# Upsampling by two: three rows moved from the third load to the first

## The chip, the cores and the metric

The kernel runs on one core of a Trainium2 chip. The metric is the device time of one execution in microseconds (us). The core has a VectorE (DVE) and a ScalarE (ACT) that compute here, a SyncE (SP) whose queue issues all transfers, a GpSimd (POOL) that only closes the program, and 16 DMA engines that carry the bytes between HBM (device memory) and the on-chip memory of 128 partitions.

## The reference

The input `x` is float32 of shape (16, 64, 64, 64). Every element is repeated twice along the height and twice along the width, so the output has shape (16, 64, 128, 128):

```python
for i in range(new_h):
    for j in range(new_w):
        result[:, :, i, j] = x[:, :, i // 2, j // 2]
```

Nothing is computed; 16.78 MB are read and 67.11 MB are written.

## The kernel before

Batch, channel and height together are 65,536 rows of 64 elements (256 B). Each of the 128 partitions takes 512 consecutive rows (`R = 512`), so in HBM a partition's input is one run of 128 KiB, and its output, four times as long, another one. One input row becomes two output rows of 128 elements, 1,024 B.

**Memory.** One tile, `mem`, holds everything in a partition: a work area at the front, of `WF` = 79 x 256 elements (room for 79 expanded rows), and behind it the whole input, `xt`, of 512 x 64 elements.

**Loads.** The input comes in three transfers on SP's queue (L195), cut at the rows `[0, HEAD, R // 2 + HEAD, R]`. With `HEAD = 32` they take 32, 256 and 224 rows of each partition: 8,192, 65,536 and 57,344 B a partition. `begin_before_barrier` moves their issue ahead of the program's start barrier.

**Chunks.** The 512 rows are expanded in nine chunks, `rows = [54, 38, 54, 61, 54, 63, 63, 63, 62]`. For each chunk VectorE copies the first `kv` rows (L213) and ScalarE the others (L214), each with a broadcast source that names every element four times; then SP issues one store of the chunk (L215). In the first chunk VectorE takes all rows but one (53 of 54), in the others about five eighths. Even chunks are expanded at the front of `mem`; odd chunks so that they end where their own source begins, over input rows that have been used up.

**What orders the work.** The program's waits are drawn from the overlap of what each step reads and writes in `mem`. The first chunk reads rows 0 to 53, which are in the first and the second load, so it waits for both. The second chunk is written over rows that the first chunk reads, so ScalarE's part of it waits for VectorE's first copy. Each later chunk waits until the store of the chunk two before it has landed, as it is expanded into the same space. The third load is first needed by the sixth chunk. All twelve transfers are on one queue, so on each DMA engine they follow each other in the order of issue: three loads, then nine stores. `close_early` lets the program's closing steps run while the last store is under way; at the very end SP waits for the last store alone.

Of the kernel before, what the change touches and what calls it, by code (L numbers as in the profile page):

```python
# [153 lines left out]
@with_exitstack  # L154
def kernel(
    ctx: ExitStack,
    tc: tile.TileContext,
    x: bass.AP,
    scale_factor: int,
    out: bass.AP,  # L160
):
    nc = tc.nc
    nc.at_finalize(begin_before_barrier)
    nc.at_finalize(close_early)
    P = nc.NUM_PARTITIONS
    s = int(scale_factor)
    B, C, H, W = x.shape
    R = B * C * H // P
    fdt = x.dtype

    xp = x.rearrange("b c h w -> (b c h) w").rearrange("(p r) w -> p r w", p=P)
    op = out.rearrange("b c (h hd) w -> (b c h) (hd w)", hd=s).rearrange(
        "(p r) w -> p r w", p=P
    )

    rows = [54, 38, 54, 61, 54, 63, 63, 63, 62]
    GROW = s * s
    FREE = 79
    WF = FREE * GROW * W
    assert sum(rows) == R
    mem_pool = ctx.enter_context(tc.tile_pool(name="mem", bufs=1))
    mem = mem_pool.tile([P, WF + R * W], fdt, name="mem")
    xt = mem[:, WF:].rearrange("p (r w) -> p r w", r=R)

    HEAD = 32
    cuts = [0, HEAD, R // 2 + HEAD, R]
    for lo, hi in zip(cuts, cuts[1:]):
        nc.sync.dma_start(out=xt[:, lo:hi], in_=xp[:, lo:hi])  # L195

    def expanded(r0, r1):
        return (
            xt[:, r0:r1].unsqueeze(2).unsqueeze(4).to_broadcast([P, r1 - r0, s, W, s])
        )  # L200

    r0 = 0
    before = (0, 0)
    for n, k in enumerate(rows):
        size = k * GROW * W
        at = 0 if n % 2 == 0 else WF + r0 * W - size
        assert at >= before[1] or at + size <= before[0]
        before = (at, at + size)
        u = mem[:, at : at + size].rearrange(
            "p (k a w b) -> p k a w b", k=k, a=s, w=W  # L210
        )
        kv = k - 1 if n == 0 else k * 5 // 8 & ~1
        nc.vector.tensor_copy(out=u[:, :kv], in_=expanded(r0, r0 + kv))  # L213
        nc.scalar.copy(out=u[:, kv:], in_=expanded(r0 + kv, r0 + k))  # L214
        nc.sync.dma_start(out=op[:, r0 : r0 + k, :], in_=u)  # L215
        r0 += k
# [35 lines left out]
```

## Time and profile before

| | |
|---|---|
| median of 3 runs | 197.04 us (196.91 to 197.17) |
| the profiled execution | 196.92 us, of which 195.6 us are the span from first to last instruction |
| VectorE | 9 copies, 52.3 us |
| ScalarE | 9 copies, 40.8 us, and a table load of 1.3 us |
| DMA | 83.89 MB in 1,728 packets, 99.2% of 16 engines' span |
| first load | issued at 0.00 us, landed after 4.7 us |
| second load | landed at 24.01 us |
| first store | issued at 38.48 us, landed at 57.30 us |

Of the 1,728 packets 192 are writes of 4 B to a semaphore, one for each of the 12 transfers on each of the 16 engines; the other 1,536 are one for each partition of each transfer, eight on each engine.

The profile is one execution, taken by the hardware profiler. "L213" is line 213 of the kernel. The page gives busy times of engines and of DMA; a row of digits cuts the span (or the window that was asked for) into 40 slices and gives the busy share of each in tenths, where 9 is 90% or more. The DMA view of a narrow window counts a packet, its bytes and its whole duration at the packet's start, so a share can be over 100%: times the window's length and 16 engines, and divided by the number of packets, it gives the mean duration of one. The chain of waits lists the work that ended last, each piece with its start and its duration in us.

### The profile page before, as it was taken

How to read it: one execution, taken by the hardware profiler on the slowest of the kernel's cores; microseconds unless marked ns; L12 is line 12 of the kernel's file. 1: busy time of each engine (PE TensorE's matmuls, PEld its weight loads, DVE VectorE, ACT ScalarE, POOL GpSimd, SP SyncE). 2: the span in 40 equal slices, each digit the busy share in tenths (PEclk: the TensorE clock that was granted, in tenths of full speed). 3: DMA queues.
4: the chain of work that ended last, by engine and by line, in shares of the span. 5: the costliest groups of instructions: out<-in, count | busy, mean ns of one | idle time of the engine just before them, and what ended most of it. 6: DMA issues, size and time to landing. Idle time of an engine off the chain costs nothing.

```text
span 195.6 us, 102 instructions
## 1 busy us (share of the span) xinstructions
DVE 52.3 (27%) x9; ACT 42.1 (21%) x10; POOL 0.2 (0%) x4
## 2 busy tenths in 40 slices
DVE  0000099940026091053008204500540073000000
ACT  2000000160029700059500004970000073000000
POOL 0000000000000000000000000000000000000000
DMA  9999989889899989999999899999999999999994
GB/s 429 429 429 429 402 375 563 375 362 543 362 436 390 555 362 418 486 409 409 409 420 532 362 531 433 422 422 422 422 422 422 422 422 422 422 435 545 467 428 208
DMA packets 1728, 83.89 MB, mean 429 GB/s; under 512 B 192, under 2 KB 192, under 8 KB 192
## 3 DMA queue, kind: packets, MB, share of 16 engines
q1 hardware_dynamic: 1728, 83.89, 99.2%
HBM read 16.78 MB, written 67.11 MB: 429 GB/s over the span
## 4 chain that ended last, share of the span: by engine, by line
DMA 65%; ACT 11%; DVE 7%; SPq 0%; issue 0%; DVEq 0%; ACTq 0%
DMA out_dram<-mem 53%; DMA mem<-in_x_dram 12%; ACT mem L214 11%; DVE mem L213 7%; SPq L195 0%; DVEq L213 0%; ACTq L214 0%; SPq L215 0%
## 5 line engine op out<-in xcount | busy, mean ns | idle before, releaser
L213 DVE COPY mem<-mem 128x9728 f32<-128x9728 f32 (+3 forms) x9 | 52.3, 5818 | 110.9 <-DMA out_dram<-mem 86.8
L214 ACT COPY mem<-mem 128x6400 f32<-128x6400 f32 (+5 forms) x9 | 40.8, 4530 | 119.4 <-DMA out_dram<-mem 84.2
L214 ACT ACT_TABLE_LOAD x1 | 1.3, 1283 | 1.7 <-PEq L233 1.7
L233 POOL MEMSET const-bfloat16-1.0<- 128x1 bf16 x1 | 0.1, 102 | 0.0
L233 POOL MEMSET const-uint8-127<- 128x1 uint8 x1 | 0.1, 102 | 0.0
L233 POOL MEMSET const-float32-1.0<- 128x1 f32 x1 | 0.1, 99 | 0.0
L233 POOL MEMSET const-float32-0.0<- 128x1 f32 x1 | 0.1, 98 | 0.2 <-issue 0.2
## 6 DMA issues: line engine op xcount, KB each, us to landing
out_dram<-mem SPq DMA_DIRECT2D x3, 8064.0 KB, 32.4
out_dram<-mem SPq DMA_DIRECT2D x3, 6912.0 KB, 22.9
out_dram<-mem SPq DMA_DIRECT2D x1, 7936.0 KB, 32.3
out_dram<-mem SPq DMA_DIRECT2D x1, 7808.0 KB, 29.3
mem<-in_x_dram SPq DMA_DIRECT2D x1, 7168.0 KB, 40.1
out_dram<-mem SPq DMA_DIRECT2D x1, 4864.0 KB, 26.7
mem<-in_x_dram SPq DMA_DIRECT2D x1, 1024.0 KB, 4.7
mem<-in_x_dram SPq DMA_DIRECT2D x1, 23.6
```

What stands on the lines that cost most here:

```text
L213: nc.vector.tensor_copy(out=u[:, :kv], in_=expanded(r0, r0 + kv))
L214: nc.scalar.copy(out=u[:, kv:], in_=expanded(r0 + kv, r0 + k))
L233: nc = _bacc.Bacc("TRN2", target_bir_lowering=False, num_devices=1)
```

## The change

The first load takes 35 rows of each partition instead of 32 (8,960 B instead of 8,192 B), the third 221 instead of 224 (56,576 B instead of 57,344 B). The second keeps its 256 rows but begins and ends three rows later in `x` and in `xt`. Copies, stores, their order and their waits are the same.

```diff
-    HEAD = 32
+    HEAD = 35
     cuts = [0, HEAD, R // 2 + HEAD, R]
     for lo, hi in zip(cuts, cuts[1:]):
         nc.sync.dma_start(out=xt[:, lo:hi], in_=xp[:, lo:hi])
```

## The prediction

> **What bounds the kernel now.** I read the page first, for the load on each resource.
>
> ```profile
> span 195.6 us, 102 instructions
> DVE 52.3 (27%) x9; ACT 42.1 (21%) x10; POOL 0.2 (0%) x4
> DMA  9999989889899989999999899999999999999994
> q1 hardware_dynamic: 1728, 83.89, 99.2%
> HBM read 16.78 MB, written 67.11 MB: 429 GB/s over the span
> ```
>
> The 16 DMA engines are busy for 99.2% of the span, all on one queue; VectorE and ScalarE are idle three quarters of the time. The kernel is bound by bytes through the DMA engines. It moves 83.89 MB before and after the change, so the time can move only if an engine runs dry, if bytes move at another rate, or if the 16 engines share the work less or more evenly. The chain of waits shows where an engine could run dry.
>
> ```profile
> 0.42 23.59 DMA mem<-in_x_dram
> ...
> 24.11 14.30 DVE mem L213
> ...
> 38.48 18.82 DMA out_dram<-mem
> ...
> 57.33 4.89 ACT mem L214
> ...
> 62.24 22.85 DMA out_dram<-mem
> ```
>
> The columns are start and duration. The second load lands at 24.01, VectorE copies 53 rows of the first chunk until 38.41 and the first store is issued at 38.48. The third load has been queued since 0.9 us and fills the DMA engines meanwhile. So the chain through VectorE is not itself the bound: it only has to deliver the first store before the engines finish the third load. How near that is, the DMA view shows in narrow windows. It books each packet at its start. First 39.6 to 41.2 (0.04 us a digit), then 1.0 to 1.5 (0.0125 us a digit), then 2.7 to 3.6.
>
> ```profile
> DMA  0000000000090099999990090900000000000000
> DMA packets 32, 0.88 MB, mean 553 GB/s; under 512 B 16, under 2 KB 16, under 8 KB 16
> ...
> DMA  9990000000900900009000000099909000900090
> q1 hardware_dynamic: 16, 0.13, 126.0%
> ...
> DMA packets 48, 0.39 MB, mean 437 GB/s; under 512 B 0, under 2 KB 0, under 8 KB 0
> q1 hardware_dynamic: 48, 0.39, 103.0%
> ```
>
> In the first window 16 packets are semaphore writes that close the third load, one on each engine, and the other 16 are the first data packets of the first store (16 x 55,296 B = 0.88 MB). The latter start between 40.04 and 40.64: 1.56 us and more after the issue at 38.48. In the second window are the first packets of the very first load, issued at 0.00 on an empty queue: from 1.00 to about 1.48 us after their issue. This is the only place where the trace shows how long an idle engine takes from issue to first packet.
>
> **The change part by part.** *The second load lands later.* Three rows more are 128 x 3 x 256 B = 98.3 KB ahead of it; at 429 GB/s that is 0.23 us. Per engine it is the same: 8 packets grow by 768 B. The landing goes from 24.01 to 24.24, VectorE's copy from 24.11 to 24.34, the first store's issue from 38.48 to 38.71. The 14.30 us of the copy stays (same rows, same shape).
>
> *The third load is shorter by the same 98.3 KB.* It starts 0.23 us later on each engine and ends where it ended: engines come free between 40.04 and 40.64 as before. The sum of load bytes, and the count of packets (three loads of 128), are unchanged: 0.
>
> *The first load's packets grow from 8,192 to 8,960 B.* The steady ones in the third window cost 1.030 x 0.9 us x 16 / 48 = 0.309 us each. The growth is in the 0.23 us already. The first packets cost 1.260 x 0.5 x 16 / 16 = 0.63 us, so 0.32 us of start-up; it falls on the first packet whatever its size, and I take no change for it. Bounds: the packet size would save or cost at most that 0.32 us.
>
> *What of the 0.23 us reaches the end?* The cover is the time between the first store being ready to start and the engines coming free. Ready is not shown by the trace, because the engines were busy. Lower bound of the cover: nothing, if a store's first packet needs the whole 1.56 us. Upper bound: a store might start as soon as SP's issue instruction of 0.35 us is done, which would leave 1.21 us at the earliest engine. The nearest row is the first load's 1.00 to 1.48. If the engine that starts first there is also the one free first here, the cover is 40.04 - 38.48 - 1.00 = 0.56 us; if the slowest one is, it is 40.04 - 38.48 - 1.48 = 0.08 us. Against 0.23 that leaves +0.33 or -0.15 us. Most engines come free later than 40.04, so I take the cover as sufficient: 0 us, and in the worst pairing 0.15 us on an engine that is early anyway.
>
> The Trainium skill ("DMA: Bandwidth & Descriptors", section "Latency and other measured facts") gives about 0.6 us to the first byte for DMAs issued from this queue. By that figure the cover would be 0.96 us, an estimate from the page; no run here shows it for a store, and the loads' 1.00 to 1.48 us is longer.
>
> An engine that does run dry pays more than its gap, if it restarts as it did at the beginning: 0.32 us. With the whole 0.23 us uncovered, that makes 0.55 us on that engine. Whether it shows at the end depends on which engine: the closing semaphore packets of the last store start between 194.77 and 195.21 (eight of 16 before 194.9, two after 195.1), so an early engine has up to 0.44 us to lose.
>
> *What is queued behind the later wait.* On SP, the second store is behind the first; it goes out when ScalarE's 3.61 us copy ends, at 42.1, now 42.3, but its packets are wanted only when the first store's are done, near 56.4: covered by 14 us. ScalarE's copy and VectorE's next one follow the first copy and move by 0.23 us under the same cover. From there every step waits for a store's landing, so it moves with the DMA queue. The least cover I find is that of the third store: issued at 62.24, and wanted when the second is done near 68, as VectorE's next copy, which waits for that landing, starts at 68.89. So 6 us. Sum: 0.00 us on the profiled execution's 196.92 us (span 195.6 and 1.3 around it), which is 0.12 below the median of the runs shown, 197.04. I carry the median over.
>
> **The rivals.**
>
> *Slower: the first store comes too late.* Place: the join of third load and first store, 40.04 to 40.64. It decides from the point where a store needs over 1.33 us (1.56 - 0.23) from issue to first packet. For it: the first load's slowest engine needed 1.48. Against it: every engine has its own time, most come free after 40.2, and the engines that finish last have up to 2.1 us. Price: 0.23 us if all engines wait and restart freely, 0.55 with the start-up of the cold packets: 197.27 to 197.59. Chance 0.17. Of that, 0.10 lies over the 0.39 us that make 0.2%.
>
> *Slower: loads at a worse offset.* The second and third load now begin 8,960 B into each partition's rows, on both sides a multiple of 256 B, no longer of 512 B. Every packet in this trace was a multiple of 512 B at such an offset, so no row prices it. The widest rate difference between packets here is that of 8,192 B in 0.309 us, 26.5 GB/s, against 27.1 for 55,296 B (window 44 to 56: 96 packets with a share of 102.0%, so 1.020 x 12 x 16 / 96 = 2.04 us each): 2.3%. Over the 36.5 us of these two loads that would be 0.84 us; 1% would be 0.37. So 197.4 to 197.88. Against it: the packets stay long and contiguous. Chance 0.16.
> The Trainium skill ("DMA: Bandwidth & Descriptors", section "How a descriptor splits into AXI transactions") says that a transfer is cut into 256-byte pieces, and that only a start off a 256-byte boundary costs extra; all starts and lengths here keep to it, so by that rule this rival's price is nothing. No row of this trace shows it.
>
> *Faster: the engines finish more evenly.* The end is set by the last of 16 engines, at 195.21, while half of them are done before 194.90: 0.31 us to be had if the start-up falls more evenly with longer first packets. The packets that run while the first store is issued cost a little more, too: about 2.14 us each on the mean (window 37.9 to 38.45: 3.883 x 0.55 x 16 / 16) where the ones before took 2.12 (35.8 to 36.4: 3.311 x 0.6 x 16 / 15), together 0.27 us, possibly on few engines; with the last one among them, up to that is saved. Taken together up to 0.58 us, so 196.46; the greater part of it is needed to pass 0.2%. For it: only the spread. Against it: nothing in the change evens anything out. Chance 0.12.
>
> *The change does nothing* is the forecast itself: three rows later and well covered. Chance 0.55.
>
> **How the numbers follow.** The likeliest case is the covered one: 197.04 us, with the runs' own 196.91 to 197.17. About 0.2%, 0.39 us, is what a measurement of this kernel can tell from no change. Faster by more takes most of the faster rival: 0.10. Slower: 0.10 from the late store and 0.14 from the offset, 0.24. Within: 0.55, 0.07 and 0.02 from the two slower rivals and 0.02 from the faster: 0.66. The range takes in the covered case, all of the late store's price and the near halves of the other two: 196.75 to 197.65, which leaves out some 0.15.
>
> **What the profile after would show.** Right: the second load's landing near 24.24, the first store's issue near 38.71, its first packets still from 40.04, each right behind the third load's last one; DMA still at 99%. Late store: a step of more than 0.1 us in the time from which those packets start, and longer first packets. Offset: the third load ends later though the store is in time, at 40.3 or beyond, and its packets take over 2.12 us x 56,576 / 57,344 = 2.09 us. Faster: closing packets nearer together and ending before 194.9. The forecast is wrong if the median leaves 196.75 to 197.65.

## The result and the profile after

The kernel takes 197.54 us after the change (median of 21 runs, 197.38 to 197.92) against 197.16 us before (21 runs beside them, 196.84 to 197.58): a ratio of 1.0019, 95% interval 1.0012 to 1.0026. It is slower by 0.2%, near the bound that the prediction named, and clear of noise. The profiled execution took 197.45 us, with a span of 196.1 us.

The page of the profile after:

```profile
span 196.1 us, 102 instructions
DMA  9999989989899989999999899999999999999994
q1 hardware_dynamic: 1728, 83.89, 99.1%
```

DMA stays the bound, on the same packets and bytes. The chain of waits after (start, duration, what):

```profile
0.42 23.91 DMA mem<-in_x_dram
...
24.43 14.30 DVE mem L213
...
38.80 18.62 DMA out_dram<-mem
...
57.44 4.89 ACT mem L214
...
62.35 22.96 DMA out_dram<-mem
```

The second load lands at 24.33 instead of 24.01 and the first store is issued at 38.80 instead of 38.48: 0.32 us later, where 0.23 was forecast. Then two windows of the DMA view after, each with its count of packets: the join of third load and first store, 39.6 to 41.2 (0.04 us a digit), and the very end, 195.3 to 195.8.

```profile
DMA  0000000000000099990999990090000000000000
DMA packets 32, 0.88 MB, mean 553 GB/s; under 512 B 16, under 2 KB 16, under 8 KB 16
...
DMA packets 2, 0.00 MB, mean 0 GB/s; under 512 B 2, under 2 KB 2, under 8 KB 2
```

The first store's packets still start between 40.1 and 40.7, so the join looks as before. But two of the 16 closing packets now start after 195.3. Before, the last two started between 195.1 and 195.3, the window of these lines:

```profile
DMA  0000000001000000000001000000000000000000
DMA packets 2, 0.00 MB, mean 0 GB/s; under 512 B 2, under 2 KB 2, under 8 KB 2
```

The two late engines of after can be followed in the trace. A packet starts where the one before it on its engine ended, within some 0.01 us, so the records can be strung into 16 chains, one an engine. Before, each engine takes 154.6 us (154.59 to 154.75) from its first store packet to its closing packet, and no engine has a gap at the join. After, 14 engines take 154.6 to 154.7 and close between 194.85 and 195.24. The other two end their third load at 40.30 and 40.47, start their first store packet only at 40.42 and 40.66, and then take 155.1 us: the 0.5 us more are spread over most of their 72 store packets, 7 ns each on the mean. They close at 195.53 and 195.75. Without them the end would be 195.24, as the 195.21 of before. So the difference of these two spans, 0.5 us, lies on two engines: a gap of 0.1 to 0.2 us at the join, and 0.5 us in small pieces over the nine stores. The medians of the two kernels are only 0.38 us apart; the profiled execution of before was one of its quicker ones.

### The profile page after: what moved, and what is told of

It reads as the page before. It is cut to its first block, busy times and chain, and to the rows that moved or that the text cites. A ratio compares the mean times of both kernels' runs of the same rounds, so it can differ in the third digit from the quotient of the medians.

```text
span 196.1 us, 102 instructions
## 1 busy us (share of the span) xinstructions
DVE 52.3 (27%) x9; ACT 42.1 (21%) x10; POOL 0.2 (0%) x4
## 4 chain that ended last, share of the span: by engine, by line
DMA 65%; ACT 11%; DVE 7%; SPq 0%; issue 0%; DVEq 0%; ACTq 0%
DMA out_dram<-mem 53%; DMA mem<-in_x_dram 12%; ACT mem L214 11%; DVE mem L213 7%; SPq L195 0%; DVEq L213 0%; ACTq L214 0%; SPq L215 0%
## 6 DMA issues: line engine op xcount, KB each, us to landing
mem<-in_x_dram SPq DMA_DIRECT2D x1, 7072.0 KB, 40.2
```

## The experiments

The runs were made in four groups, each with its own runs of the kernel before, whose medians were 197.38 to 197.44 us; the row "after" is the result above, beside 197.16 us. So the ratios carry the comparison, not the medians. "Stretch" is by how much the last packet of the third load is longer than the others of its size, mean of 16 engines. "Slow" counts the engines that take over 154.85 us from first store packet to close. Both are from the one profiled execution of each kernel. In e5 and e9 the chains of several engines run so close together that they can be confused, and the count is rough; the sum over all engines is not affected, and there it is 5.2 and 5.0 us over 16 x 154.59, that of ten engines with 0.5 us each.

The expectations call an engine dry that finished its third load before the first store's packet was at hand; such an engine shows a gap. A slow engine need not show one (e9).

| kernel | first store issued, us | stretch, us | slow | median, us | ratio to before (95%) |
|---|---|---|---|---|---|
| 52 rows on VectorE (e11) | 31.57 | 0.91 | 0 | 198.35 | 1.0053 (1.0040 to 1.0067) |
| 49 rows, HEAD 32 (e7) | 37.59 | 0.46 | 0 | 198.00 | 1.0029 (1.0018 to 1.0041) |
| 49 rows, HEAD 35 (e6) | 37.72 | 0.60 | 0 | 197.77 | 1.0019 (1.0010 to 1.0028) |
| HEAD 22 (e13) | 37.80 | 0.45 | 0 | 197.55 | 1.0007 (0.9998 to 1.0016) |
| 51 rows, HEAD 35 (e1) | 38.27 | 0.04 | 0 | 197.30 | 0.9996 (0.9987 to 1.0006) |
| one-row pieces (e8) | 38.31 | 0.18 | 0 | 197.34 | 0.9996 (0.9986 to 1.0005) |
| HEAD 29 (e3) | 38.42 | 0.02 | 0 | 197.16 | 0.9993 (0.9981 to 1.0005) |
| HEAD 30 (e14) | 38.47 | 0.02 | 0 | 197.11 | 0.9988 (0.9979 to 0.9997) |
| before (HEAD 32) | 38.48 | 0.02 | 0 | | 1 |
| larger first load alone (e10) | 38.55 | 0.00 | 0 | 197.39 | 1.0004 (0.9995 to 1.0013) |
| three-row pieces (e12) | 38.74 | 0.01 | 6 | 197.62 | 1.0014 (1.0005 to 1.0023) |
| after (HEAD 35) | 38.80 | 0.01 | 2 | 197.54 | 1.0019 (1.0012 to 1.0026) |
| after again (e5) | 38.89 | 0.00 | 10 | 197.70 | 1.0019 (1.0010 to 1.0028) |
| later landing alone (e9) | 39.02 | 0.00 | 11 | 197.56 | 1.0013 (1.0004 to 1.0022) |
| HEAD 48 (e4) | 39.91 | 0.00 | 16 | 197.70 | 1.0015 (1.0006 to 1.0024) |
| one row again (e2) | 41.76 | 0.00 | 16 | 199.62 | 1.0113 (1.0099 to 1.0127) |

**The change kept, the store early again (e1).**

```diff
-    HEAD = 32
+    HEAD = 35
-        kv = k - 1 if n == 0 else ...
+        kv = k - 3 if n == 0 else ...
```

> The change kept (HEAD = 35), but VectorE gives two more rows of the first chunk to ScalarE (51 and 3 of 54 instead of 53 and 1), so that its copy is 2 x 0.27 = 0.54 us shorter and the first store is issued near 38.26, earlier than before the change (38.48). Theory LATE (the first store reaches some DMA engines after they have finished the third load): no engine runs dry, time as in the quicker executions before, 197.0 us, 0.2% under after's 197.54. Theory OFFSET (loads that begin at 8,960 B move slower): nothing is undone, 197.5 us. Theory START (a first load of larger packets starts up worse): 197.5 us too.

Measured 197.30 us, 0.9996 of before, with no slow engine: the loss of the change is gone although its loads are kept, which speaks against OFFSET and START. It is not as fast as LATE expected. In its profile one engine's last load packet is 0.33 us longer than usual, and that engine closes last.

**A delay without a change of the loads, first try (e2).**

```diff
         nc.vector.tensor_copy(out=u[:, :kv], in_=expanded(r0, r0 + kv))
+        if n == 0:
+            nc.vector.tensor_copy(out=u[:, kv - 1 : kv], in_=expanded(r0 + kv - 1, r0 + kv))
```

> The loads of before (HEAD = 32); VectorE copies the last of its 53 rows of the first chunk a second time, 256 elements, which delays the first store by some 0.3 us and changes no load. Whether this short copy runs ahead of the second chunk's depends on the order of issue in VectorE's queue; the first store waits for the one that writes its rows. LATE: as after, 197.5 us, with a gap in front of the first store's packets on some engines; if the short copy is queued behind the second chunk's, the store is 3 us later and the time 199 to 200 us. OFFSET and START: 197.1 us, as before.

The short copy came behind the second chunk's, so the store was issued at 41.76, after the third load was over. Measured 199.62 us, as foreseen for that order. It shows an idle engine's start, in the windows 40.2 to 42.6 and 42.6 to 42.8 of the DMA view:

```profile
DMA packets 16, 0.00 MB, mean 0 GB/s; under 512 B 16, under 2 KB 16, under 8 KB 16
...
DMA packets 16, 0.88 MB, mean 4424 GB/s; under 512 B 0, under 2 KB 0, under 8 KB 0
```

In the first only the 16 packets that close the third load; all 16 first store packets are in the second, 0.85 to 0.99 us after the issue. Each engine took 155.1 us from there. The first store packet itself took 2.07 to 2.09 us instead of 2.04.

**The second load earlier (e3).**

```diff
-    HEAD = 32
+    HEAD = 29
```

> HEAD = 29: second load three rows earlier than before, first store near 38.25, offset 7,424 B, again a multiple of 256 B and not of 512 B. LATE: 197.0 us, and without the executions of 197.4 us and more that before has in a third of its runs. OFFSET: 197.5 us. START: 197.0 us or a little less, so LATE and START are not told apart by this one.

Measured 197.16 us, no slow engine. Nine of 11 runs lie at 197.05 to 197.23; two (197.71 and 198.22) stay unexplained. An offset of 7,424 B costs nothing.

**The second load much later (e4).**

```diff
-    HEAD = 32
+    HEAD = 48
```

> HEAD = 48: second load 16 rows later than before, which is 1.2 us; first store near 39.7; offset 12,288 B, a multiple of 4 KiB. LATE: all 16 engines run dry, those that waited 0.1 to 0.2 us after the change now wait 1.1 us, and the time is 198.4 us or more (after's 197.54 plus 13 rows x 0.076 us). OFFSET: 197.1 us, as before, since the offset is even. START: between 197.1 and 197.5 us, scaled by the size of the first packets up to 198.

All 16 engines run dry, as LATE says, but the time is 197.70 us and not 198.4. Three windows of the DMA view of this kernel, 40.2 to 40.75, 40.75 to 41.0 and 195.7 to 196.1:

```profile
DMA packets 16, 0.00 MB, mean 0 GB/s; under 512 B 16, under 2 KB 16, under 8 KB 16
...
DMA packets 16, 0.88 MB, mean 3539 GB/s; under 512 B 0, under 2 KB 0, under 8 KB 0
...
DMA packets 16, 0.00 MB, mean 0 GB/s; under 512 B 16, under 2 KB 16, under 8 KB 16
```

The third load closes before 40.75 on all engines, the first store packets start between 40.76 and 40.94, and the end is between 195.80 and 196.07: 155.0 to 155.15 us on every engine. The packets start 0.85 to 1.03 us after the issue at 39.91, so the gaps are 0.03 to 0.67 us, largest on the engines that were free first. The expectation had counted on from after's gaps as if those had been set by the time to start; they were not, for 38.80 + 1.03 is 39.83, before any engine of after was free.

**The change again (e5), its loads with five rows on ScalarE (e6), and before's with five rows (e7).** e5 is the change as it stands; the others:

```diff
-        kv = k - 1 if n == 0 else ...
+        kv = k - 5 if n == 0 else ...
```

> The change as it is (HEAD = 35), beside the next three on one chip. Theory DRY, formed from the traces so far: a DMA engine that finishes its third load without the first store's packet at hand pays the gap and, after it, some 0.5 us more over its nine stores (from its first store packet to the end it took 155.1 us instead of 154.6); the time is that of the last engine. Here 1 to 4 of 16 engines run dry, the first store is issued near 38.8 and the time is 197.5 us. Theory OFFSET, the rival: the engines take 154.6 us each and the loads end later.

> The loads of the change (HEAD = 35), with five rows of the first chunk on ScalarE, so 49 on VectorE and the first store issued near 37.7. DRY: no engine runs dry, each takes 154.6 us from its first store packet to the end, and the time is 0.2 to 0.4 us under that of the change: 197.1 to 197.3 us. OFFSET: as the change, 197.5 us.

> The loads of before (HEAD = 32), 49 rows of the first chunk on VectorE: first store near 37.4. DRY: no engine runs dry, and the slower part of before's executions (197.3 to 197.6) is gone: median 197.1 us, and the same as HEAD = 35 with 49 rows within 0.15 us. OFFSET: as before with its spread, and 0.4 us faster than HEAD = 35 with 49 rows.

e5 came out at 197.70 us, with some ten slow engines, more than expected. e6 and e7 are misses: no engine is slow, each takes 154.6 us, and yet they are as slow as the change or slower, 1.0019 and 1.0029. The price is at another place. The window 37.9 to 38.7 holds the start of the third load's last packet on each of the 16 engines; before, then e6:

```profile
DMA packets 16, 0.92 MB, mean 1147 GB/s; under 512 B 0, under 2 KB 0, under 8 KB 0
q1 hardware_dynamic: 16, 0.92, 267.0%
```

```profile
DMA packets 16, 0.91 MB, mean 1132 GB/s; under 512 B 0, under 2 KB 0, under 8 KB 0
q1 hardware_dynamic: 16, 0.91, 335.8%
```

The share times 0.8 us is the mean duration: 2.136 us before, 2.686 in e6, whose packets are even a little smaller. Its other packets of the same size take 2.088. So with the store issued early the last load packet in front of it is longer, by 0.6 us on the mean.

**A delay in pieces (e8).**

```diff
-        nc.vector.tensor_copy(out=u[:, :kv], in_=expanded(r0, r0 + kv))
+        for a, b in [(0, 47), *((a, a + 1) for a in range(47, 53))] if n == 0 else [(0, kv)]:
+            nc.vector.tensor_copy(out=u[:, a:b], in_=expanded(r0 + a, r0 + b))
```

> The loads of before (HEAD = 32), but VectorE's first copy is cut into one of 47 rows and six of one row, which costs only time, so that the first store is issued 0.2 to 0.4 us later, near 38.8 as with the change. DRY: as the change, 197.5 us, with 1 to 4 engines dry. OFFSET: as before, 197.1 to 197.4 us.

A miss of the edit, not of the theory: the one-row copies start 0.20 us apart, faster than a row within the long copy (0.27), so the store was issued earlier, at 38.31. It tells of the early side only, with a stretch of 0.18 us in an execution of 197.52 us; the median, 197.34 us, is as before's.

**The two parts of the change, each alone (e9, e10).**

```diff
-    cuts = [0, HEAD, R // 2 + HEAD, R]
+    cuts = [0, 32, 291, 512]   # e9: the second load is longer
+    cuts = [0, 35, 288, 512]   # e10: the first load is longer
```

> One part of the change alone, the later landing: the first load keeps its 32 rows, the second takes 259 (it then goes as two pieces a partition, some 0.07 us more), so it lands 0.23 to 0.3 us later than before, and the first store is issued near 38.8. Theory TWO-SIDED, formed from the runs so far: at the join of third load and first store each engine pays one of two prices. If the store is there early (issued at 37.6 to 37.7), the last packet of the third load is stretched, by 0.5 to 0.6 us on the mean of 16 engines; if it is late, an engine runs dry and its nine stores take 155.1 instead of 154.6 us; between, near 38.4, both are small. TWO-SIDED: the late price, 197.5 to 197.7 us, with engines at 155.1. START (the cost is in the larger first load): as before, 197.1 to 197.4.

> The other part alone, the larger first load: 35, 253 and 224 rows, so that the second lands when it did before and the first store is issued near 38.5. TWO-SIDED: as before, 197.1 to 197.4 us. START: as the change, 197.5 to 197.7.

e9: 1.0013, some 11 slow engines, a loss as with the change. e10: 1.0004, none slow, as before, though its second load begins at 8,960 B as in the change. The closing packets from 195.3 to 195.9, in e9 and then in e10:

```profile
DMA packets 12, 0.00 MB, mean 0 GB/s; under 512 B 12, under 2 KB 12, under 8 KB 12
...
DMA packets 1, 0.00 MB, mean 0 GB/s; under 512 B 1, under 2 KB 1, under 8 KB 1
```

The later landing carries the loss; the size of the first load and the offset carry none. (e9 is not the later landing quite alone: its second load goes as 256 packets of 33,152 B instead of 128. e12 below leaves all loads as they were.) In e9 the gaps at the join add up to 0.2 us over all 16 engines, on three of them, while the time after it adds up to 5.0 us too much. So most of the slow engines there show no gap: a late store makes engines slow, but a visible gap is not the condition for it.

**What stretches the load's last packet (e11).**

```diff
-        kv = k - 1 if n == 0 else ...
+        kv = k - 2 if n == 0 else ...
```

> The loads of before; VectorE copies 52 rows of the first chunk, an even number, which it does at twice the rate (about 7.1 us, as its 32- and 38-row copies show), so that the first store is issued near 31.3 and VectorE's and ScalarE's copies of the second chunk are over by 35. Two rivals inside TWO-SIDED. QUEUE: what stretches the third load's last packet is the store's packet waiting behind it on the engine: the last packets are stretched by 0.5 us and more, though no copy runs beside them, and the time is 197.7 us or more. COPIES: what stretches them is the copying of the second chunk beside them: no stretch at the join, some in the packets of 31 to 35 us, and the time is 197.1 us or under.

Measured 198.35 us. The timeline of this kernel, 23 to 46 us, then its window 38 to 38.8 of the DMA view:

```profile
24.39 10.09 DVE L213 COPY mem<-mem 128x13312 f32<-128x13312 f32 x2 [24.39 <-DMA mem<-in_x_dram]
31.56 3.61 ACT L214 COPY mem<-mem 128x4096 f32<-128x4096 f32 x1 [6.63 <-DVE mem L213]
31.57 3.97 SPq L215 DMA_DIRECT2D out_dram<-mem  x2
```

```profile
DMA packets 16, 0.92 MB, mean 1147 GB/s; under 512 B 0, under 2 KB 0, under 8 KB 0
q1 hardware_dynamic: 16, 0.92, 378.3%
```

All copies are over by 35.2, and the packets that ran beside them are not longer than 2.14 us. The last ones, with nothing beside them but the store in the queue, take 3.783 x 0.8 = 3.03 us instead of 2.12: a stretch of 0.91. That is QUEUE, and COPIES has fallen.

**A delay without a change of the loads (e12).**

```diff
-        nc.vector.tensor_copy(out=u[:, :kv], in_=expanded(r0, r0 + kv))
+        parts = [0, 41, 44, 47, 50, 53] if n == 0 else [0, kv]
+        for a, b in zip(parts, parts[1:]):
+            nc.vector.tensor_copy(out=u[:, a:b], in_=expanded(r0 + a, r0 + b))
```

> The loads of before; VectorE's first copy is cut into one of 41 rows and four of 3 rows, at the slow rate as before, each costing some 0.13 us more, so that the first store is issued near 39.0 and no load is changed. TWO-SIDED: more than four engines dry (155.1 us over the nine stores), none of the last load packets stretched, 197.5 to 197.8 us. OFFSET (loads that begin at 8,960 B are slower): as before, 197.1 to 197.4.

The store was issued at 38.74, a little less late than planned. Measured 197.62 us, ratio 1.0014, with six slow engines, which close after 195.4 (window 195.4 to 195.9 of the DMA view):

```profile
DMA packets 6, 0.00 MB, mean 0 GB/s; under 512 B 6, under 2 KB 6, under 8 KB 6
```

The loads are those of before. A later store without any change of the loads makes the loss of the change; OFFSET has fallen.

**Only the loads moved, to both places (e13, e14).**

```diff
-    HEAD = 32
+    HEAD = 22   # e13
+    HEAD = 30   # e14
```

> Only the loads move: HEAD = 22, second load ten rows earlier than before (0.76 us), copies as before, first store issued near 37.7. TWO-SIDED: the early price, as with 49 rows on VectorE: last packets of the third load stretched by 0.4 to 0.6 us on the mean, no engine dry, 197.6 to 198.0 us. Rival LATE-ONLY (only a late store costs, and the slow times with 49 and 52 rows came from the changed copies): 197.0 to 197.2 us.

> Only the loads move: HEAD = 30, first store issued near 38.35 to 38.45, between the two prices. TWO-SIDED: last packets stretched by under 0.1 us on the mean, no engine dry, 197.0 to 197.2 us, 0.1 to 0.3 us under before's median, which mixes executions on both sides of the late edge. LATE-ONLY: the same, 197.0 to 197.2 us.

The last load packets of e13 (window 37.8 to 38.7) and of e14 (37.9 to 38.7):

```profile
q1 hardware_dynamic: 16, 0.96, 295.5%
```

```profile
q1 hardware_dynamic: 16, 0.93, 269.3%
```

e13: 2.955 x 0.9 = 2.66 us where its other packets take 2.21, a stretch of 0.45, with the copies unchanged. Its time, 197.55 us, is a little under the expected 197.6; against before the interval holds 1 (0.9998 to 1.0016), but 0.4 us over e14 in the same group. LATE-ONLY, which said 197.0 to 197.2, has fallen. e14: 2.693 x 0.8 = 2.15 us, no engine slow, 197.11 us: 0.9988 of before, interval 0.9979 to 0.9997. It is faster than before by 0.1%, and by its ratio faster than the change too, beside which it did not run. In its profile the store is issued at 38.47 as in before's (38.48), but its third load is longer: the engines come free 1.93 to 2.36 us after the issue, in before 1.56 to 2.13. That speaks for this time, and not the issue by itself, as what places a kernel between the prices.

## Why the prediction was wrong

**What bounds the kernel** was right: bytes through DMA, unchanged, and the time moved by two of the three ways that the prediction left open: engines ran dry at the join of third load and first store, and, for the larger part, bytes then moved more slowly on the engines that were hit. The median, 197.54 us, lies within the stated range, because the range took in the price of a late store. The forecast itself, a covered delay that changes nothing, was wrong: the interval of the ratio leaves out 1. Of the 0.50 us between forecast and median, 0.12 is the median of before, carried over from three runs; 21 runs gave 197.16.

**The later landing.** Right in kind; 0.32 us instead of 0.23 at the issue. Why is not known: executions with the very same loads differ as much. With before's loads the first copy starts at 24.11 in before, and at 24.13 to 24.39 in e2, e7, e8, e11 and e12.

**The step that failed** is "What of the 0.23 us reaches the end?", where the cover was taken as sufficient. It took the cover as the time between the moment at which an idle engine could start the store and the moment at which the busy one comes free. That moment is now measured: 0.85 to 1.03 us after the issue (e2, e4), even better than the 1.00 to 1.48 us of the first load that the prediction used. The Trainium skill's 0.6 us to the first byte ("DMA: Bandwidth & Descriptors", section "Latency and other measured facts") is less than any engine here needed from the start of the issue. Counted from the end of SP's issue instruction, which takes 0.33 us, they needed 0.52 to 0.70 us, and by that count it would agree. By the measured 1.03 us after had cover left on all engines, and yet two of them ran dry with the store issued 1.50 and 1.67 us before they came free. In the profiles with all engines at 154.6 to 154.8 us every engine came free at least 1.56 us after the issue; below some 1.9 us an engine may or may not be hit (after, e5, e9, e12; none in before and e10). So a busy engine needs the next transfer earlier than an idle one could begin it, and before, with 1.56 to 2.13 us, had no cover to give.

**The price of a hit engine.** The rival of the late store had the right place, and its 197.27 to 197.59 takes in the measured time, but partly by luck. It reckoned 0.55 us on an engine: a gap of 0.23 and a restart of 0.32 on the first packet, after the cold start of the loads. Measured, the first packet costs 0.02 to 0.05 us (e2, e4), the gap in after is 0.1 to 0.2, and 0.5 us come in small pieces over the following stores (155.1 instead of 154.6 us). The sum of 0.6 to 0.7 us is more than the 0.44 us which the prediction granted an early engine to lose, so two engines sufficed to move the end.

**The other rivals.** The offset costs nothing: in the window 7 to 21 us the second load's packets take 0.961 x 14 x 16 / 89 = 2.42 us before and 0.885 x 14 x 16 / 82 = 2.42 us after, and e10 and e12 separate the offset from the loss. That agrees with the Trainium skill's rule that only a start off a 256-byte boundary costs extra ("DMA: Bandwidth & Descriptors", section "How a descriptor splits into AXI transactions"). The engines did not finish more evenly.

**What was missing** is that the store can also be too early. The prediction's list of what the change moves had only one edge; the runs have two, at about 38.3 and 38.6 us for the issue by one profile of each kernel, with before between them and near the late one. Before's own runs spread from 196.84 to 197.80 in all groups, from e14's times to after's, which would fit a kernel whose executions fall on both sides of the late edge. The spread of the landing would suffice: a copy that starts at 24.39 instead of 24.11 would put before's store at 38.76 (an estimate), where e12's was, with six slow engines. That is argued: no slower execution of before was profiled.

**Open**: why an engine that the first store reaches late stays slower for 150 us, also where no gap shows, why a waiting store makes the load packet ahead of it longer, and which of the engines are hit. The runs fix when it happens and what it costs, not the mechanism in the DMA engine.

## What to carry to other kernels

Where loads and stores follow each other on one saturated queue, look at the join engine by engine: 99% busy before and after hid a loss on two of 16 engines, which the closing packets of the last transfer gave away. Do not take "an idle engine could have started by then" as cover for a busy one; leave it what the engines here needed, some 2 us from issue to need, and test a row or two to either side, because too early a store costs as well. When the time is the last engine's, price a stall by what that engine loses to the end, not by its gap.

## What the runs showed of the hardware

- A store that waits behind a load on the same queue lengthens that load's last packet: by 0.02 us on the mean of 16 engines when issued at 38.4 to 38.5, by 0.04 and 0.18 at 38.3, by 0.45 to 0.60 at 37.6 to 37.8 and by 0.91 at 31.6, there without a copy beside it. From store to store nothing of the kind shows (in before, e6 and e11 the last packets of a store are within 0.01 us of its others).
- A DMA engine that ran dry at that join takes 155.1 instead of 154.6 us for the 72 store packets that follow (all 16 in e2 and e4). With a late store engines without a visible gap are slowed too (e9).
- An idle engine starts a store 0.85 to 1.03 us after its issue (e2, e4). A busy one was left with a gap when it came free 1.50 and 1.67 us after it (after).
- VectorE copies 53 rows in 14.29 us and 52 rows in 7.09 us (e11): the odd count of the first chunk runs at half the rate. Here that delays the first store to the place where neither price is paid; the even count, 7 us sooner on VectorE, makes the kernel 0.5% slower.
